# A decoder step's expert mixer: the last token block by gathered value rows in place of a dense product

## The chip, the cores and the metric

The kernel runs on one core of a Trainium2 chip. The metric is the device time of one execution in microseconds (us); the median of several runs counts. The profile's span, from the first to the last instruction, leaves out what lies around it.

## The reference, cut to what matters

One layer of a hybrid decoder: differential attention and an mLSTM mix the tokens (512 prompt tokens and 8 sample tokens), and a PEER layer follows, which is what the change touches. For each token 8 heads pick 16 of 16,384 experts each, by a product of two key halves:

```python
eidx = jnp.take_along_axis(cidx, pos, axis=-1)      # i1 * 128 + i2, 8 heads x 16
g = jax.nn.softmax(top_s, axis=-1)
ue = u[eidx]
ve = v[eidx]
act = jax.nn.gelu(jnp.einsum('nd,nhkd->nhk', xb, ue))
return jnp.einsum('nhk,nhkd->nd', g * act, ve)
```

So every token has 128 selected rows of `u` and of `v` (1024 floats each) and one weight, g * act, for each row of `v`. `v` is 16,384 x 1024 floats, 64 MB. The output is the residual plus the weighted sum of the token's 128 rows of `v`.

## The kernel before, in words

The 512 prompt tokens are two halves of 256, and each half is two blocks of 128 tokens: A0, A1, B0 and B1. For every block the kernel picks the experts (`scores`), gathers the rows of `u` one selection at a time (`gather_dot`: 128 indirect transfers from the POOL queue, each fetching one row for every token, 512 KB, with a product and sum on VectorE), and turns the dots into the weights `S` (`gelu_w`). It does not gather rows of `v`. `w_block` instead builds, for each block, the dense matrix of weights, experts x tokens, from one-hot products on VectorE, GpSimd, ScalarE and TensorE (32 groups of four tokens), into two `WT` tiles of 64 x 128 floats per partition. `v_part(j, ...)` then loads the chunk of 128 rows number j of `v` (512 KB, queue of SyncE, tag "v" with VB = 5 buffers) and multiplies the matching slice of each block's matrix with it, two matmuls of 128x512 for each block, accumulated over the 128 chunks in PSUM. With `split` False the matmuls take fp32 operands. With `split` True chunk and weights are taken apart into a rounded part and a remainder (`vh`, `vl` on ScalarE and VectorE in the buffers of `ring`; `wh`, `wl` likewise) and three products of reduced precision are summed: six matmuls for each block.

The order: chunks 0 to 127 serve A0 and A1 in fp32, and the last 28 (from JB = 100) B0 too. Beside them the `u` rows of B0 and B1 are gathered. `v_done` adds a block's PSUM sums to the residual and stores it. Then `w_block` builds B1's matrix, in the `WT` buffers that A's matrices leave, while B0 takes chunks 0 to 19 (NF = 20); chunks 20 to 99 serve B0 and B1, chunks 100 to 127 and then 0 to 19 only B1, all split. `sample_peer` is a generator whose steps (one gather or so each) are strewn among the chunks: 8 gathers of `u` rows (`urow_s`), each with a broadcast load (`xb`), then 8 gathers of `v` rows (`vrow_s`) with matmuls on 8-column weights (`py_s`); all of these tiles are in `ring`.

The engines' queues are filled by a scheduler, which simulates the program: on each engine the earliest instruction of the program that is ready in that simulation goes next. Each engine then runs its own list in order. Dependences and buffer releases become semaphore waits. `dps` holds eight PSUM banks: two for `pst_d`, two for each accumulator (`v_acc`).

Of the kernel before, what the change touches and what calls it, by code (L numbers as in the profile page):

```python
# [5 lines left out]
F32 = mybir.dt.float32  # L6
F32R = mybir.dt.float32r
BF16 = mybir.dt.bfloat16
I32 = mybir.dt.int32
U32 = mybir.dt.uint32  # L10
AF = mybir.ActivationFunctionType
ALU = mybir.AluOpType
# [3 lines left out]
P = 128  # L16
D = 1024
# [4 lines left out]
HALF = 256  # L22
# [12 lines left out]
JB = 100  # L35
# [7 lines left out]
NF = 20  # L43
# [15 lines left out]
def step_kernel(  # L59
# [7 lines left out]
    nc = tc.nc  # L67
# [8 lines left out]
    u_rows, v_rows = peer_u[0], peer_v[0]  # L76
# [24 lines left out]
    def ctile(shape, name, dt=F32, pool=None):  # L101
        return (pool or consts).tile(shape, dt, name=name)

    ident = ctile([P, P], "ident")
# [25 lines left out]
    def pst(tag):  # L130
        return ps.tile([P, 512], F32, tag=tag, name=f"ps_{tag}", bufs=PB[tag])
# [7 lines left out]
    def act(out, in_, func, scale=1.0, bias=None, accum=None):  # L139
        kw = {}  # L140
        if accum is not None:
            kw["accum_out"] = accum
        n = out.shape[0]
        b = (zero if bias is None else bias)
        nc.scalar.activation(out, in_, func, bias=b[:n, 0:1] if b.shape[0] != n else b, scale=scale, **kw)

    def copy(out, in_, scale=1.0):
        nc.scalar.activation(out, in_, AF.Copy, scale=scale)  # L148
# [6 lines left out]
    for tok, rows, sample in ((0, P, False), (P, P, False), (0, NS, True)):  # L155
        t = tp.tile([P, D], F32, tag="r4", name="xin", bufs=R4B)
# [57 lines left out]
    for i in range(2):  # L214
        scr = sp.tile([P, 64], F32, tag="w1", name="lscr", bufs=W1B)
        nc.vector.scalar_tensor_tensor(scr, lamt[:, 2 * i, :], 1.0, lamt[:, 2 * i + 1, :], op0=ALU.mult,
                                       op1=ALU.mult, accum_out=lam[:, i:i + 1])
# [7 lines left out]
    for c in range(2):  # L225
        raw = sp.tile([P, P], F32, tag="w1", name="skraw", bufs=W1B)
        nc.sync.dma_start(raw, peer_subkeys[0, c])
        p = pst("t")
# [905 lines left out]
    def w_new(*pools):  # L1134
        return [(pool.tile([P, JH, P], F32, tag="WT", name="WT", bufs=2), JH * i) for i, pool in enumerate(pools)]

    def w_prep(sel, pool, pst_):
        out = []
        for key in ("i1", "i2", "S"):
            p = pst_()  # L1140
            nc.tensor.transpose(p[:, 0:P], sel[key], ident)
            t = pool.tile([P, P], BF16 if key == "i1" else F32, tag=f"T_{key}", name=f"T_{key}", bufs=1)
            copy(t, p[:, 0:P])
            out.append(t)
            if key == "i2":
                t = pool.tile([P, P], F32, tag="T_n2", name="T_n2", bufs=1)
                copy(t, p[:, 0:P], scale=-1.0)
                out.append(t)
        return out
# [3 lines left out]
    def w_block(sel, wT, pool, pst_, no):  # L1153
        ONA, PM = ONAS[no], PMS[no]
        if not iota4:
            t = pool.tile([P, P, TG], BF16, name="iota4")
            nc.vector.tensor_copy(t, iota.unsqueeze(2).to_broadcast([P, P, TG]))
            iota4.append(t)
        i1T, i2T, ni2T, sT = w_prep(sel, pool, pst_)
        for g in range(P // TG):  # L1160
            t0 = g * TG
            tg = slice(t0, t0 + TG)
            e = pool.tile([P, P, TG], BF16, tag="ohe", name="ohe", bufs=OHE)
            nc.vector.tensor_tensor(e, iota4[0], i1T[:, tg].unsqueeze(1).to_broadcast([P, P, TG]), op=ALU.is_equal)
            a = pool.tile([P, TG, P], F32, tag="oh1", name="oh1", bufs=OH1)
            sb = sT[:, tg].unsqueeze(2).to_broadcast([P, TG, P])
            nc.gpsimd.tensor_mul(a[:, :PM], e.rearrange("p j t -> p t j")[:, :PM], sb[:, :PM])  # L1167
            if PM < TG:
                nc.vector.tensor_mul(a[:, PM:], e.rearrange("p j t -> p t j")[:, PM:], sb[:, PM:])
            b = pool.tile([P, TG, P], F32, tag="oh2", name="oh2", bufs=OHB)  # L1170
            for t in range(ONA):
                act(b[:, t, :], iota, AF.Abs, bias=ni2T[:, t0 + t:t0 + t + 1])
            if ONA:
                nc.scalar.activation(b[:, 0:ONA, :], b[:, 0:ONA, :], AF.Relu, bias=one, scale=-1.0)
            if ONA < TG:
                n = TG - ONA
                nc.vector.tensor_tensor(b[:, ONA:TG, :], iota.unsqueeze(1).to_broadcast([P, n, P]),
                                        i2T[:, t0 + ONA:t0 + TG].unsqueeze(2).to_broadcast([P, n, P]), op=ALU.is_equal)
            pw = pst_().rearrange("p (t j) -> p t j", t=TG)
            for t in range(TG):  # L1180
                nc.tensor.matmul(pw[:, t, :], b[:, t, :], a[:, t, :], start=True, stop=True)  # L1181
            for w, j0 in wT:
                copy(w[:, :, t0:t0 + TG], pw[:, :, j0:j0 + w.shape[1]].rearrange("p t j -> p j t"))
# [3 lines left out]
    for hf in range(2):  # L1187
# [24 lines left out]
        else:  # L1212
            actx.close()
            wr = ctx.enter_context(tc.tile_pool(name="wright", bufs=1, side="right"))
# [42 lines left out]
    wt = dctx.enter_context(tc.tile_pool(name="wt", bufs=1, side="right"))  # L1257
    dps = dctx.enter_context(tc.tile_pool(name="dpsum", bufs=1, space=PSUM))

    selA, selB = halves[0][0], halves[1][0]  # L1260

    def pst_d():
        return dps.tile([P, 512], F32, tag="pw", name="ps_w", bufs=2)
# [4 lines left out]
    dp = dctx.enter_context(tc.tile_pool(name="dense", bufs=2))  # L1268

    def v_acc(b):  # L1270
        return [dps.tile([P, 512], F32, tag=f"y{b}{q}", name=f"y{b}{q}") for q in range(2)]

    def v_part(j, use, split):
        vt = dp.tile([P, D], F32, tag="v", name="vtile", bufs=VB)
        nc.sync.dma_start(vt, v_rows[j * P:(j + 1) * P])
        ws = [next(w[:, j - j0, :] for w, j0 in wT if j0 <= j < j0 + w.shape[1]) for _, wT, _, _ in use]
        pairs = [((w, vt),) for w in ws]
        if split:
            vh, vl = (ring.tile([P, D], F32R, tag="g", name=n) for n in ("vh", "vl"))
            wh, wl = (dp.tile([P, 2, P], F32R, tag="wh", name=n, bufs=3) for n in ("wh", "wl"))  # L1280
            copy(vh, vt)
            nc.vector.tensor_sub(vl, vt, vh.bitcast(F32))  # L1282
            for b, w in enumerate(ws):
                copy(wh[:, b, :], w)
                nc.vector.tensor_sub(wl[:, b, :], w, wh[:, b, :].bitcast(F32))  # L1285
            pairs = [((wh[:, b, :], vh), (wh[:, b, :], vl), (wl[:, b, :], vh)) for b in range(len(ws))]
        for (py, _, j0, j1), pp in zip(use, pairs):
            for i, (lw, rv) in enumerate(pp):
                for q in range(2):
                    nc.tensor.matmul(py[q], lw, rv[:, q * 512:(q + 1) * 512],  # L1290
                                     start=(j == j0 and i == 0), stop=(j == j1 and i == len(pp) - 1))

    def v_done(tok, py):
        t = dp.tile([P, D], F32, tag="v", name="x1r", bufs=VB)
        nc.sync.dma_start(t, scr_x1[tok:tok + P])
        for q in range(2):
            nc.vector.tensor_add(t[:, q * 512:(q + 1) * 512], t[:, q * 512:(q + 1) * 512], py[q])
        nc.sync.dma_start(y_prompt[0, tok:tok + P], t)
# [59 lines left out]
    yB0 = v_acc(2)  # L1358
    useB0 = (yB0, wB0, JB % P, (JB - 1) % P)
    for j in range(JB, P):  # L1360
        v_part(j, useA + [useB0], False)
    for b in range(2):
        v_done(b * P, useA[b][0])
    wB1 = w_new(wr, wt)
    w_block(selB[1], wB1, wr, pst_d, 3)
    useB1 = (v_acc(0), wB1, NF % P, (NF - 1) % P)
    for j in range(NF):
        v_part(j, [useB0], True)
    for j in [*range(NF, P), *range(NF)]:
        v_part(j, ([useB0] if NF <= j < JB else []) + [useB1], True)  # L1370
        if j == JB - 1:
            v_done(HALF, yB0)
        if j >= SST[1] and j % SST[2] == 0:
            next(steps, None)
    for _ in steps:
        pass
    v_done(HALF + P, useB1[0])
    dctx.close()
    ctx.close()

# [30 lines left out]
```

## Time and profile before

| | us |
|---|---|
| median of 3 runs | 2348.86 |
| lowest and highest run | 2343.86 and 2352.1 |
| span of the profiled execution | 2338.3 |
| median above that span | 10.6 |
| TensorE busy in the span | 2136.7 (91%) |
| VectorE, GpSimd, ScalarE busy | 1676.6, 1247.0, 815.3 |

No device time beside its span is given for the profiled execution, so the runs stand beside it: their median is 10.6 us longer than the span. The windows view splits the span by time and tells which engine is full where. PE is TensorE's matmuls, PEld its weight loads, DVE VectorE, ACT ScalarE, POOL GpSimd, SP SyncE. An instruction's "busy" of many pipelined matmuls is the union of their spans; the distance between starts tells the pace.

### The profile page before, as it was taken

The page shows a single profiled execution, that of the slowest core. Times are in us where ns is not written, and L with a number is a line of the kernel's source. Part 1 is how long each engine was busy: PE and PEld are TensorE (multiplying, and loading weights), DVE is VectorE, ACT ScalarE, POOL GpSimd, SP SyncE. Part 2 cuts the span into 40 slices and gives each one's busy share as a digit, 9 for nine tenths or more (in the row PEclk, how much of TensorE's full clock was granted, in tenths as well). Part 3 has the DMA queues.
Part 4 walks back from the last instruction along what each step waited for, and adds up shares of the span by engine and source line. Part 5 has one row for each costly group of instructions (what it writes and reads, how often), then busy time and mean ns, then how long its engine had stood idle before and what let it go on. Part 6 is the DMA issues. An engine that isn't in the chain of part 4 may idle for free. (4 is left out here: it accounts for less than half of the span.)

```text
span 2338.3 us, 28902 instructions
## 1 busy us (share of the span) xinstructions
PE 2136.7 (91%) x8921; PEld 1528.1 (65%) x8921; DVE 1676.6 (72%) x3820; ACT 815.3 (35%) x2055; POOL 1247.0 (53%) x1118
## 2 busy tenths in 40 slices
PE   6999899889999999998979569999999997899998
PEld 4776678777878777787758454444555446777765
DVE  2355666785899878668978985664797759766667
ACT  4334233213355323333334770000122005454556
POOL 0588863551876557657785785441688636200001
PEclk9999999999989999999979669999999999999999
DMA  5687767887888989998883189997998974567678
GB/s 165 202 277 237 231 222 230 287 288 268 305 300 304 303 309 346 353 369 290 309 280 132 41 281 367 409 409 283 352 353 317 409 304 155 184 221 231 219 266 283
DMA packets 282253, 648.38 MB, mean 277 GB/s; under 512 B 29774, under 2 KB 155786, under 8 KB 282098
## 3 DMA queue, kind: packets, MB, share of 16 engines
q0 software_dynamic: 94464, 343.97, 40.9%
q1 hardware_dynamic: 187634, 302.55, 38.3%
q8 instruction: 71, 1.16, 0.2%
q14 instruction: 84, 0.69, 0.1%
HBM read 628.25 MB, written 18.18 MB: 276 GB/s over the span
## 5 line engine op out<-in xcount | busy, mean ns | idle before, releaser
L1102 POOL DMA_INDIRECT urow<-in_peer_u,k_e x512 | 621.1, 1213 | 336.8 <-DVE urow L1108 240.0
L1108 DVE SCALAR_TENSOR_TENSOR urow<-urow,xn 128x1024 f32<-128x1024 f32 x512 | 646.7, 1276 | 152.5 <-DMA urow<-in_peer_u,k_e 146.7
L1290 PE MATMUL y<-vtile,WT 128*128 128x512 f32 x1136 | 494.0, 595 | 1.7 <-ACT WT L148 0.9
L288 PE MATMUL ps_mm<-x,wch 128*128 128x264 f32 (+1 forms) x1536 | 385.3, 404 | 26.1 <-DVE sig L312 17.9
L1290 PEld LDWEIGHTS y<-vtile,WT 128*128 128x128 f32 x1136 | 215.1, 191 | 265.3 <-issue 263.5
L288 PEld LDWEIGHTS ps_mm<-x,wch 128*128 128x128 f32 x1536 | 301.0, 201 | 82.5 <-DVE sig L312 21.2
L148 ACT ACTIVATE vh<-vtile 128x1024 fp32r<-128x1024 f32 x148 | 155.6, 1057 | 228.7 <-DMA vtile<-in_peer_v 123.4
L1282 DVE TENSOR_TENSOR vl<-vtile,vh 128x1024 fp32r<-128x1024 f32 x148 | 182.7, 1240 | 39.8 <-ACT vh L148 37.8
L831 POOL TENSOR_TENSOR kpage<-kpage,qb 128x1024 f32<-128x1024 f32 x64 | 150.1, 2357 | 72.2 <-DMA qb<-scr_q 63.4
L288 PE MATMUL ps_mm<-hT,wch 128*128 128x256 f32 (+1 forms) x768 | 185.1, 392 | 1.8 <-DVE sig L312 0.9
L1167 POOL TENSOR_TENSOR oh<-ohe,T_S 128x512 f32<-128x512 bf16 (+2 forms) x128 | 148.1, 1162 | 70.9 <-ACT T_S L148 35.7
L1181 PE MATMUL ps_w<-oh,oh 128*128 128x128 f32 x768 | 122.8, 317 | 63.9 <-POOL oh L1167 29.2
L1181 PEld LDWEIGHTS ps_w<-oh,oh 128*128 128x128 f32 x768 | 113.6, 225 | 84.3 <-POOL oh L1167 63.9
L288 PEld LDWEIGHTS ps_mm<-hT,wch 128*128 128x128 f32 x768 | 144.1, 194 | 24.8 <-issue 1.3
L293 PE MATMUL ps_mm<-wch,x 128*128 128x256 f32 (+1 forms) x640 | 148.2, 382 | 0.3 <-DVE kS L690 0.3
L1290 PE MATMUL y<-vl,wh 128*128 128x512 f32 x456 | 140.2, 398 | 7.1 <-DVE vl L1282 6.1
L1290 PE MATMUL y<-vh,wh 128*128 128x512 f32 x456 | 140.1, 397 | 1.9 <-ACT vh L148 1.8
L819 POOL DMA_INDIRECT vpage<-in_cache_v,kidx x64 | 80.6, 1259 | 109.8 <-DVE vacc L897 64.2
L1290 PE MATMUL y<-vh,wl 128*128 128x512 f32 x456 | 133.3, 402 | 1.7 <-DVE wl L1285 1.7
L293 PEld LDWEIGHTS ps_mm<-wch,x 128*128 128x128 f32 (+1 forms) x640 | 106.2, 171 | 29.7 <-issue 2.4
L897 DVE SCALAR_TENSOR_TENSOR vacc<-vpage,aS,vacc 128x128 f32<-128x128 f32 x384 | 112.1, 363 | 18.7 <-DMA vpage<-in_cache_v,kidx 18.2
L148 ACT ACTIVATE WT<-ps_w 128x256 f32<-128x256 f32 x192 | 62.7, 379 | 151.6 <-PE ps_w L1181 151.6
(419 smaller groups left out, 3098.4 us busy)
## 6 DMA issues: line engine op xcount, KB each, us to landing
vtile<-in_peer_v SPq DMA_DIRECT2D x276, 512.0 KB
wch<-in_w_in SPq DMA_DIRECT2D x256, 256.0 KB
wch<-in_peer_wq SPq DMA_DIRECT2D x64, 256.0 KB
wch<-in_w_branch_a SPq DMA_DIRECT2D x32, 256.0 KB
wch<-in_w_branch_b SPq DMA_DIRECT2D x32, 256.0 KB
wch<-in_w_out SPq DMA_DIRECT2D x32, 256.0 KB
urow<-in_peer_u,k_e POOLq DMA_INDIRECT x512, 7.6
qb<-scr_q SPq DMA_DIRECT2D x8, 512.0 KB
```

Of the source, the lines that this page charges most:

```text
L148: nc.scalar.activation(out, in_, AF.Copy, scale=scale)
L288: nc.tensor.matmul(out, w[:, c0:c0 + m], xk[:, :n], start=(k == 0 and i == 0), stop=(k == KT - 1 and i == len(tt) - 1))
L293: nc.tensor.matmul(out, x[:, k, t0:t0 + m], ch[k // KP][:, k % KP, :n], start=(k == 0), stop=(k == KT - 1))
L819: nc.gpsimd.indirect_dma_start(out=t, out_offset=None, in_=rows, in_offset=bass.IndirectOffsetOnAxis(ap=kidx[:, b * 8 + pg:b * 8 + pg + 1] ...
L831: (nc.vector if KDV and pg % KDV == KDV - 1 else nc.gpsimd).tensor_mul(kt, kt, qb)
L897: nc.vector.scalar_tensor_tensor(acc[:, h, :], vt[:, h, :], wa, acc[:, h, :], op0=ALU.mult, op1=ALU.add)
L1102: nc.gpsimd.indirect_dma_start(out=gt, out_offset=None, in_=u_rows, in_offset=bass.IndirectOffsetOnAxis(ap=d["e"][:, k:k + 1], axis=0))
L1108: d["dot"] = nc.vector.scalar_tensor_tensor(gt, gt, 1.0, xn2, op0=ALU.mult, op1=ALU.mult, accum_out=d["S"][:, k:k + 1])
L1167: nc.gpsimd.tensor_mul(a[:, :PM], e.rearrange("p j t -> p t j")[:, :PM], sb[:, :PM])
L1181: nc.tensor.matmul(pw[:, t, :], b[:, t, :], a[:, t, :], start=True, stop=True)
L1282: nc.vector.tensor_sub(vl, vt, vh.bitcast(F32))
L1290: nc.tensor.matmul(py[q], lw, rv[:, q * 512:(q + 1) * 512], start=(j == j0 and i == 0), stop=(j == j1 and i == len(pp) - 1))
```

## The change

B1 gets no dense matrix. `vg_prep` clears a tile `wz` of 128 x 4096 floats, computes the expert number i1 * 128 + i2 in floats, transposes it and `S` on TensorE, and writes the transposed weights on a stride of 33 into `wz`, so that `wz` holds for each token t a 128x32 weight tile that is zero except in column t mod 32. `vg_run` makes 32 groups; a group gathers for four tokens (i, 32 + i, 64 + i, 96 + i) their 128 selected rows of `v`, one indirect transfer of 512 KB for each token, and multiplies each by the token's 128x32 weights into the 32 PSUM partitions 32j to 32j + 31, in two matmuls of 512 columns. The gathered rows go into 12 slots of 128x1024 in two slabs, which take the buffers of `WT` that A leaves, as B1's matrix did before; the first four slots' room is `wz`. B0 takes its chunks 0 to 99 alone and in fp32 (`split` False), one group after every third chunk.

```diff
+    def vg_prep(d, pool, wz):
+        nc.gpsimd.memset(wz, 0.0)
+        ef = pool.tile([P, P], F32, name="vg_ef", bufs=1)
+        nc.vector.scalar_tensor_tensor(ef, d["i1"], 128.0, d["i2"], op0=ALU.mult, op1=ALU.add)
+        p = pst_d()
+        nc.tensor.transpose(p[:, 0:P], ef, ident)
+        nc.tensor.transpose(p[:, P:2 * P], d["S"], ident)
+        eT = pool.tile([P, P], I32, name="vg_eT", bufs=1)
+        nc.vector.tensor_copy(eT, p[:, 0:P])
+        for j in range(4):
+            copy(wz[:, j * 1024:(j + 1) * 1024:33], p[:, P + 32 * j:P + 32 * j + 32])
+        return wz.rearrange("p (t c) -> p t c", c=32), eT
+
+    def vg_run(prep, py, slots):
+        wz, eT = prep
+        for i in range(32):
+            gts = []
+            for j in range(4):
+                t = 32 * j + i
+                gt = slots()
+                nc.gpsimd.indirect_dma_start(out=gt, out_offset=None, in_=v_rows,
+                                             in_offset=bass.IndirectOffsetOnAxis(ap=eT[:, t:t + 1], axis=0))
+                gts.append((j, t, gt))
+            for q in range(2):
+                for j, t, gt in gts:
+                    nc.tensor.matmul(py[q][32 * j:32 * j + 32, :], wz[:, t, :], gt[:, q * 512:(q + 1) * 512],
+                                     start=(i == 0), stop=(i == 31), skip_group_check=True)
+            yield
...
-    wB1 = w_new(wr, wt)
-    w_block(selB[1], wB1, wr, pst_d, 3)
-    useB1 = (v_acc(0), wB1, NF % P, (NF - 1) % P)
-    for j in range(NF):
-        v_part(j, [useB0], True)
-    for j in [*range(NF, P), *range(NF)]:
-        v_part(j, ([useB0] if NF <= j < JB else []) + [useB1], True)
-        if j == JB - 1:
-            v_done(HALF, yB0)
+    slab = [pool.tile([P, 8, D], F32, tag="WT", name="vslab", bufs=2) for pool in (wr, wt)]
+    slot_i = [0]
+
+    def slots():
+        i = 4 + slot_i[0] % 12
+        slot_i[0] += 1
+        return slab[i // 8][:, i % 8, :]
+
+    yB1 = v_acc(0)
+    run = vg_run(vg_prep(selB[1], dp, slab[0][:, 0:4, :].rearrange("p a c -> p (a c)")), yB1, slots)
+    for j in range(JB):
+        v_part(j, [useB0], False)
+        if j % 3 == 2:
+            next(run, None)
         if j >= SST[1] and j % SST[2] == 0:
             next(steps, None)
+    v_done(HALF, yB0)
+    for _ in run:
+        pass
     for _ in steps:
         pass
-    v_done(HALF + P, useB1[0])
+    v_done(HALF + P, yB1)
```

## Rows read from the trace of the kernel before

**Rows 1.** Windows of the last 430 us: busy us (instructions), clock, DMA share, GB/s.
```profile
1908.00:1924.00 16.00, 16.00 (x39) 7.15 (x38) 4.00 (x8) 2.73 (x4) 0.00 (x0) 1.00 0.37 125
1930.00:2010.00 80.00, 58.78 (x362) 50.28 (x363) 78.06 (x95) 43.25 (x102) 48.92 (x32) 1.00 0.42 142
2010.00:2290.00 280.00, 269.38 (x1123) 206.77 (x1122) 179.19 (x323) 147.77 (x291) 14.17 (x13) 1.00 0.71 236
2290.00:2338.30 48.30, 42.63 (x160) 27.07 (x158) 33.76 (x50) 27.82 (x45) 4.09 (x3) 0.98 0.79 279
```

**Rows 2.** Matmul groups of the whole span: records | busy us, mean ns.
```profile
L1290 PE MATMUL y<-vtile,WT 128*128 128x512 f32 x1136 | 494.0, 595 | 1.7 <-ACT WT L148 0.9 <-DMA vtile<-in_peer_v 0.8
...
L1290 PE MATMUL y<-vl,wh 128*128 128x512 f32 x456 | 140.2, 398 | 7.1 <-DVE vl L1282 6.1 <-ACT vh L148 0.9
...
L1337 PE MATMUL py_s<-vrow_s,wz 128*8 128x512 f32 x32 | 15.1, 593 | 6.1 <-DMA vrow_s<-in_peer_v,eT 6.1
```

**Rows 3.** Timeline at 2150 us, split chunks of two blocks: start, us, instruction.
```profile
2149.66 1.06 ACT L148 ACTIVATE vh<-vtile 128x1024 fp32r<-128x1024 f32 x1 [1.35 <-PE y L1290]
...
2152.46 1.06 ACT L148 ACTIVATE vh<-vtile 128x1024 fp32r<-128x1024 f32 x1 [1.34 <-PE y L1290]
```

**Rows 4.** Timeline at the end of A's chunks and the start of B1's matrix.
```profile
1913.10 0.19 PEld L1290 LDWEIGHTS y<-vtile,WT 128*128 128x128 f32 x1 [0.24 <-issue]
1913.53 0.19 PEld L1290 LDWEIGHTS y<-vtile,WT 128*128 128x128 f32 x1 [0.24 <-issue]
...
1923.83 1.02 PE L1290 MATMUL y<-vtile,WT 128*128 128x512 f32 x2
...
1926.86 0.29 DVE L1129 TENSOR_TENSOR k_S<-k_e,k_g 128x128 f32<-128x128 f32 x1
...
1929.18 0.26 ACT L148 ACTIVATE T_S<-ps_w 128x128 f32<-128x128 f32 x1
...
1930.89 1.06 ACT L148 ACTIVATE vh<-vtile 128x1024 fp32r<-128x1024 f32 x1 [1.45 <-DMA vtile<-in_peer_v]
```

**Rows 5.** Windows of two earlier stretches with gathers and chunks together.
```profile
1500.00:1600.00 100.00, 100.00 (x234) 44.27 (x233) 59.83 (x99) 0.00 (x0) 45.47 (x50) 1.00 1.03 409
1700.00:1750.00 50.00, 50.00 (x189) 28.18 (x188) 46.90 (x69) 14.51 (x48) 41.14 (x35) 1.00 0.97 352
```

**Rows 6.** DMA view of 1500 to 1600 us: queues, then issues.
```profile
q0 software_dynamic: 7012, 25.53, 63.9%
q1 hardware_dynamic: 4207, 15.32, 38.5%
...
vtile<-in_peer_v SPq DMA_DIRECT2D x29, 512.0 KB
urow<-in_peer_u,k_e POOLq DMA_INDIRECT x50, 10.7
```

**Rows 7.** Gathers of u rows and the indices they read, by line.
```profile
L1102 POOL DMA_INDIRECT urow<-in_peer_u,k_e x512: 932/976/8858, 595.1 to 1898.9; - x171
...
DMA to landing us min/median/max: 4.1/7.6/13.5
```

**Rows 8.** The line that writes the indices: first and last start.
```profile
L1018 DVE SCALAR_TENSOR_TENSOR k_e<-k_i x32: 148/167/1048, 593.8 to 1347.8; 128x16 int32<-128x16 f32 x32
```

**Rows 9.** Timeline of PE in the attention: 64-row and 128-row matmuls in turn.
```profile
158.11 0.48 PE L738 MATMUL ps_s<-kc,qn 64*128 64x128 f32 x2
158.53 0.33 PE L741 MATMUL ps_s<-bias,identr 128*128 128x128 f32 x1
158.79 0.48 PE L738 MATMUL ps_s<-kc,qn 64*128 64x128 f32 x2
...
159.37 1.41 PE L768 MATMUL ps_a<-dg,sc 128*128 128x128 f32 x8
160.62 0.68 PE L347 MATMUL ps_t<-sq,bones 128*128 128x264 f32 x2
```

**Rows 10.** Timeline of a sample matmul among the chunks.
```profile
2288.89 1.88 PE L1337 MATMUL py_s<-vrow_s,wz 128*8 128x512 f32 x4 [0.44 <-DMA vrow_s<-in_peer_v,eT]
2290.70 0.74 PE L1290 MATMUL y<-vh,wl 128*128 128x512 f32 x2
```

**Rows 11.** Timeline of the last instructions.
```profile
2329.09 1.28 DVE L1297 TENSOR_TENSOR x1r<-x1r,y 128x512 f32<-128x512 f32 x2 [3.25 <-PE y L1290]
...
2334.84 0.31 SPq L1344 DMA_DIRECT2D out_y_sample<-x1s  x1
```

**Rows 12.** GpSimd's clears at the kernel's start.
```profile
L105 POOL MEMSET ident<- 128x128 f32 x1 | 0.2, 205 | 0.3 <-POOLq L1399 0.3
...
L1399 POOL MEMSET const-float32-0.0<- 128x1 f32 x1 | 0.1, 99 | 0.3 <-issue 0.3
```

## The prediction

> **What bounds the kernel now.** I read the windows first, then the matmul groups, the timeline where A ends, and the DMA view of the gather stretch.
>
> The change works in the last 430 us, and that stretch has two parts [rows 1]. From 1930 to 2010 us VectorE is full (78 of 80 us): it builds B1's one-hot matrix while TensorE is busy for 59 us and the DMA engines for 0.42 of the time. From 2010 to 2290 us TensorE is full (269 of 280 us), and the DMA engines move 236 GB/s at a share of 0.71. So the tail is first bound by VectorE and then by TensorE; memory is not its limit.
>
> The pace of the two kinds of products is read from starts. An fp32 matmul of 512 columns leaves two records: 128 x 4 + 28 x 2 = 568 calls in the code, 1136 records [rows 2]. Their weight loads start 0.429 us apart [rows 4], so one fp32 matmul takes 0.858 us and a chunk of one block 1.716 us. A split chunk of two blocks takes 2.80 us, from one `vh` to the next [rows 3], which is 1.40 us for each block and chunk. The dense tail is 228 such (128 for B1, 100 for B0): 228 x 1.40 = 319 us. With the matrix's stretch and the sample's matmuls this fills the 414 us from the end of A (1924 us, where its last fp32 matmul ends [rows 4]) to the end.
>
> What memory can do is seen earlier: from 1500 to 1600 us, 50 gathers and 29 chunk loads run together at 409 GB/s with all 16 engines full [rows 5, 6]. 524,288 bytes by 409 GB/s are 1.282 us for one transfer of 512 KB, of either kind.
>
> **The change part by part.** Removed: `w_block` for B1 and with it some 80 us in which TensorE had B0's 20 split chunks (28 us) to do beside the matrix; B1's 128 split chunks (179 us of TensorE); 148 chunk loads' worth of `vh`/`vl` work on ScalarE and VectorE.
>
> B0's 100 chunks become fp32: 100 x 1.716 = 172 us of TensorE in place of 140, a loss of 32 us on that engine. Nothing hides it where TensorE is the bound; where transfers are, it is free. It needs no `ring` buffers, so the sample's gathers no longer queue behind them.
>
> Added on DMA: 128 gathers. After A the list is: about 96 of the 100 chunks (some four will have come by then; before, the fourth was taken up at 1930.89 [rows 4]), 128 gathers, 24 transfers of the sample (8 `urow_s`, 8 `xb`, 8 `vrow_s`), and 4 for the two `v_done` of B: 252 x 1.282 = 323 us. Before, it was 148 + 24 + 4.
>
> Their start: the gathers need the expert numbers, and these share a PSUM tile with the transpose of `S`, which is complete at 1927.15 [rows 4]. Before, the transposed `T_S` came out at 1929.2 to 1929.4 by the same steps, so the first gather goes out at about 1929.5. The clear of `wz` is 4096 floats on GpSimd; from the 128-float and the 1-float clear, (205 - 99) / 127 = 0.83 ns a float, about 3.5 us [rows 12]. It can begin when A's last tile is free and ends at about 1927, hidden behind the wait for `S`; if not, at most 3.5 us are added. The strided copies, five of 32 to 128 columns, I put at one `T_S` copy each (0.26 us), 1.3 us beside the first gathers' landing of 4.1 us at least [rows 7]. GpSimd needs 0.98 us for a gather at the median, 144 x 0.98 = 141 us: no bound. One gather lands in 7.6 us at the median and 13.5 at most [rows 7]; with 12 slots and some 9 us for a group's turn on TensorE, 128 gathers need 128 / 12 x 22.5 = 240 us by their latency, less than 323. Nor does a slot wait for its whole slab: gathers began at 595.1 us while their index tile was still being written in slices up to 1347.8 [rows 7, 8].
>
> Added on TensorE: 256 fp32 matmuls on 32 weight columns, in groups of eight. No matmul in the trace writes upper PSUM partitions beside another, so their overlap is not seen. Bounds for a group: if they do not overlap, 16 passes at the pace of the 8-column sample matmuls, (2290.70 - 2288.89) / 4 = 0.4525 us [rows 10], 7.2 us; if four run at once, a quarter of 8 x 0.858, 1.7 us. I take 9 x 0.429 = 3.9 us: passes start in order, and the second pass of one matmul must follow its first in the same columns, so only the second pass of one and the first of the next can run side by side. This is an assumption, not a row.
>
> The price of going between tile shapes can be read where 64-row matmuls alternate with 128-row ones: the 64-row pair takes 0.42 us and the next one 0.26, against 0.31 and 0.16 at the pace of eight equal 128-row records, (160.62 - 159.37) / 8 [rows 9]: 0.21 us in and out, 32 x 0.21 = 7 us. The Trainium skill, "TensorEngine Tiling (Array Packing)", Key Properties, says that changing the tiling mode drains TensorE, which speaks against strewing the groups among full-width chunks; the rows agree in sign and give the price used here. The same page's Overview has up to four times the speed at 32 columns; by that the group takes 1.7 us and the sum below would not change, as transfers bound it.
>
> TensorE's sum after 1924 us: 172 + 32 x 3.9 (124) + the sample's 32 passes x 0.4525 (14.5) + 7 + some 4 us of waiting for the first chunks = 321 us, to 2245. Transfers: 1929.5 + 323 = 2252.5. The two are 8 us apart, so transfers are the bound by a little, and TensorE's in-order list will cost some of each: I allow 5 us. At the end: one group (3.9), the residual's additions (1.3 [rows 11]), and the store, as long as from the issue of the last one to the end of the span, 2338.3 - 2334.8 = 3.5 us [rows 11]: 9 us. Span: 2252.5 + 5 + 9 = 2267, against 2338.3. The median of the runs stands 10.6 us above the span, and I carry that over: 2278 us, 71 us or 3.0% less. (A measurement of this kernel tells about 0.3%, 7 us, from no change.)
>
> DMA has a rule that speaks against this: the Trainium skill, "DMA: Bandwidth & Descriptors", Specifications, gives about 358 GB/s as the HBM limit for one core. By that 252 transfers would take 369 us and the time would be about 2324. Rows 5 and 6 disagree: 409 GB/s held for 100 us with the same mix.
>
> Stretches before 1924 us should keep their times: the change adds nothing to them, and the buffers that it takes are those that B1's matrix took.
>
> **The rivals.**
>
> *B: transfers slower, or not mixed.* Between 1700 and 1750 us the DMA engines were full (0.97) at only 352 GB/s [rows 5]: then 252 x 1.489 = 375 us, 1929.5 + 375 + 9 + 10.6 = 2324. The limit in the second rule above would come to the same. Or the planner lets B0's fp32 chunks go ahead (172 us bound by TensorE) and leaves most gathers and the sample's transfers after them (152 x 1.282 = 195 us): 1929.5 + 172 + 195 + 9 + 10.6 = 2316. For it: the queues' order is planned on a simulation. Against: the program puts a group after every third chunk, and the 12 slots let gathers run ahead.
>
> *C: the column tiles do not overlap.* Then a group is 7.2 us, TensorE's sum 172 + 232 + 14.5 + 7 + 4 = 429 us, and the end 1924 + 429 + 5 + 10.6 = 2369 us, slower by 0.9%. At the full-width pace and with no price for the shapes (6.9 us a group, 220 us) it is 2346, no change. The point from which it decides is about 7 us for a group. For it: the 8-column sample matmuls are no faster than full ones, and each group reads four different moving tiles. Against: the four matmuls write different PSUM partitions with weights in different columns.
>
> *D: the columns overlap fully.* TensorE then falls to 172 + 55 + 26 = 253 us, and the transfers bind alone: 2258 to 2272. It is within the forecast's own range.
>
> **How the numbers follow.** Forecast with D: 0.60, own range 2258 to 2300 (the upper end is a group of 5 us with both limits in each other's way). B: 0.17, 2300 to 2335. C: 0.23, of which 0.06 is within 0.3% and 0.17 slower. Faster 0.60 + 0.17 = 0.77, same 0.06, slower 0.17. The range reaches from 2256 (252 transfers at the forecast's rate with no allowance, a shorter tail) up to 2350, which takes in B and the mild end of C; about 0.05 lies below and 0.15 above.
>
> **What would show it.** Right: DMA share near 1 and about 400 GB/s from 1935 us to some 10 us before the end, TensorE at 90% or a little more; no one-hot work after 1927; `y<-vtile` pairs at 0.43 us a record; a group's eight matmuls in about 4 us. Wrong: groups of 7 us with TensorE full and DMA at 0.7 (C); DMA full at 350, or chunks first and gathers alone at the end (B); gathers that start well after 1930; any shift of the end of A from 1924 us.

## The result, and the profile after

The changed kernel takes 2289.05 us (median of 5 runs, 2279.21 to 2292.88) against 2348.86 us (5 runs): a ratio of 0.9748, 95% interval 0.972 to 0.9775, 60 us less. The forecast was 2278 with an own range of 2258 to 2300; it lies 11 us too low. The profiled execution took 2279.21 us with a span of 2277.5, so only 1.7 us lie around a span. One run in this document, of the turned kernel of experiment 6 (2327.08 us), fell in a slower state of the chip, and its median and ratio leave it out.

The same windows as in [rows 1], after the change (busy us and instructions of PE, PEld, DVE, ACT, POOL; clock; DMA share; GB/s):

```profile
1930.00:1950.00 20.00, 13.01 (x30) 3.38 (x29) 2.44 (x6) 0.00 (x0) 11.84 (x12) 0.91 1.01 396
1950.00:2050.00 100.00, 97.31 (x274) 26.36 (x275) 8.04 (x25) 1.20 (x4) 54.61 (x57) 1.00 1.03 408
2050.00:2150.00 100.00, 97.61 (x324) 27.79 (x321) 0.00 (x0) 0.00 (x0) 51.73 (x56) 1.00 1.03 409
2150.00:2200.00 50.00, 48.67 (x153) 14.74 (x151) 0.00 (x0) 0.00 (x0) 15.13 (x17) 1.00 0.94 368
2200.00:2250.00 50.00, 50.00 (x118) 22.18 (x117) 0.00 (x0) 0.00 (x0) 0.00 (x0) 1.00 0.87 304
2250.00:2277.50 27.50, 21.48 (x51) 9.18 (x49) 2.48 (x4) 0.00 (x0) 0.00 (x0) 0.93 0.72 258
```

VectorE's and ScalarE's work is gone from the tail. From 1950 to about 2180 us the DMA engines are full at 408 to 409 GB/s, as forecast. From 2200 us they are not (0.87, then 0.72), and TensorE is full: the last 80 us or so are a stretch of another kind, where the forecast had the DMA engines full to some 10 us before the end.

The matmul groups and gathers after 1930 us (records | busy us, mean ns | idle before, releasers), which stand where [rows 2] had the split products:

```profile
L1290 PE MATMUL y<-vtile,WT 128*128 128x512 f32 x397 | 185.0, 606 | 1.2 <-DMA vtile<-in_peer_v 1.2
L1318 PE MATMUL y<-vslab 128*32 128x512 f32 x512 | 138.6, 601 | 12.2 <-DMA vslab<-in_peer_v,vg_eT 12.2
L1313 POOL DMA_INDIRECT vslab<-in_peer_v,vg_eT x128 | 122.2, 955 | 106.2 <-DMA vslab<-in_peer_v,vg_eT 47.7 <-PE y L1318 22.6 <-issue 20.7
```

Of the transfers of 512 KB after 1930 us, the DMA view counts these two kinds first; with 16 of the sample's and 4 of the two `v_done` they are 245:

```profile
vtile<-in_peer_v SPq DMA_DIRECT2D x97, 512.0 KB
vslab<-in_peer_v,vg_eT POOLq DMA_INDIRECT x128, 13.3
```

138.6 us for 32 groups are 4.3 us a group, near the 3.9 of the prediction. The timeline shows that this is a coincidence (start, us, records in a row):

```profile
2055.46 1.98 PE L1290 MATMUL y<-vtile,WT 128*128 128x512 f32 x4
2057.37 1.94 PE L1318 MATMUL y<-vslab 128*32 128x512 f32 x16
2059.24 1.98 PE L1290 MATMUL y<-vtile,WT 128*128 128x512 f32 x4
2061.16 2.26 PE L1318 MATMUL y<-vslab 128*32 128x512 f32 x12
2064.08 1.90 PE L1318 MATMUL y<-vslab 128*32 128x512 f32 x4 [0.67 <-DMA vslab<-in_peer_v,vg_eT]
2065.92 1.98 PE L1290 MATMUL y<-vtile,WT 128*128 128x512 f32 x4
2067.83 1.90 PE L1318 MATMUL y<-vslab 128*32 128x512 f32 x4
2069.67 1.98 PE L1290 MATMUL y<-vtile,WT 128*128 128x512 f32 x4
2071.58 1.92 PE L1318 MATMUL y<-vslab 128*32 128x512 f32 x8
2073.43 1.98 PE L1290 MATMUL y<-vtile,WT 128*128 128x512 f32 x4
```

A token is four records. Where none waits for a gather, four tokens together (x16) take 1.87 us to the next start, two (x8) 1.85, one (x4) 1.84: the column tiles overlap in full, and a token alone costs as much as four. The scheduler strews single tokens between the chunks, and the tokens of a longer run come apart when their gathers land one after another (12 records from 2061.16 to 2064.08 us); both raise the average to 4.3. A chunk beside a token takes 1.91 us in place of 1.716. And twelve tokens go by while five chunks do; the program has nine chunks to twelve tokens. So the gathers are done early, as the end of the timeline and of the chain of waits show:

```profile
2189.69 1.98 PE L1290 MATMUL y<-vtile,WT 128*128 128x512 f32 x4
2191.61 2.43 PE L1318 MATMUL y<-vslab 128*32 128x512 f32 x12
2193.97 77.52 PE L1290 MATMUL y<-vtile,WT 128*128 128x512 f32 x180
```

```profile
2136.43 14.60 DMA vslab<-in_peer_v,vg_eT
2158.17 14.60 DMA vslab<-in_peer_v,vg_eT
2194.04 72.31 PE y L1290 x168
2266.37 4.50 DMA x1r<-scr_x
```

In the chain a gather's landing stands every 21.7 us: 12 gathers and 5 chunks, 17 x 1.282 = 21.8 us, so this part is bound by transfers. After 2194 us TensorE has 45 chunks left (180 records in 77.52 us, 1.72 us a chunk), and the DMA engines wait for it.

### The profile page after: what moved, and what is told of

Read it like the earlier page. It is cut to its first block, busy times and chain, and to the rows that moved or that the text cites. A ratio compares the mean times of both kernels' runs of the same rounds, so it can differ in the third digit from the quotient of the medians.

```text
span 2277.5 us, 26092 instructions
## 1 busy us (share of the span) xinstructions
PE 2098.4 (92%) x8208; PEld 1349.4 (59%) x8208; DVE 1403.7 (62%) x3382; ACT 593.5 (26%) x1615; POOL 1327.5 (58%) x1215
## 4 chain that ended last, share of the span: by engine, by line
PE 44%; DVE 11%; DMA 10%; issue 7%; POOL 5%; ACT 1%; DVEq 0%; POOLq 0%; ACTq 0%
PE y L1290 20%; PE ps_mm L288 9%; DMA vslab<-in_peer_v,vg_eT 6%; DVE urow L1108 3%; POOL urow L1102 3%; PE ps_mm L293 3%; PE y L1318 3%; PE ps_s L738 2%; DMA urow<-in_peer_u,k_e 1%; PE ps_w L1181 1%; POOL oh L1167 1%; PE ps_s L741 1%; DVE tk_w L975 1%; DVE ohe L1164 1%; DMA vpage<-in_cache_v,kidx 1%
## 5 line engine op out<-in xcount | busy, mean ns | idle before, releaser
L1102 POOL DMA_INDIRECT urow<-in_peer_u,k_e x512 | 632.2, 1235 | 326.9 <-DVE urow L1108 223.3
L1290 PE MATMUL y<-vtile,WT 128*128 128x512 f32 x1536 | 680.6, 598 | 3.0 <-DMA vtile<-in_peer_v 2.1
L1290 PEld LDWEIGHTS y<-vtile,WT 128*128 128x128 f32 x1536 | 286.6, 191 | 382.5 <-issue 377.8
L1313 POOL DMA_INDIRECT vslab<-in_peer_v,vg_eT x128 | 122.2, 955 | 106.2 <-DMA vslab<-in_peer_v,vg_eT 47.7
L1318 PE MATMUL y<-vslab 128*32 128x512 f32 x512 | 138.6, 601 | 12.2 <-DMA vslab<-in_peer_v,vg_eT 12.2
L1181 PE MATMUL ps_w<-oh,oh 128*128 128x128 f32 x512 | 88.3, 336 | 46.0 <-POOL oh L1167 29.2
L1181 PEld LDWEIGHTS ps_w<-oh,oh 128*128 128x128 f32 x512 | 81.4, 242 | 62.3 <-POOL oh L1167 45.5
L1167 POOL TENSOR_TENSOR oh<-ohe,T_S 128x384 f32<-128x384 bf16 (+2 forms) x96 | 96.4, 1011 | 12.7 <-ACT T_S L148 5.6
L1318 PEld LDWEIGHTS y<-vslab 128*32 128x32 f32 x512 | 30.7, 109 | 112.0 <-issue 88.5
L832 DVE TENSOR_REDUCE sK<-kpage 128x16 f32<-128x1024 f32 x64 | 77.1, 1210 | 26.3 <-POOL kpage L831 26.2
```

The source lines that it names most:

```text
L1102: nc.gpsimd.indirect_dma_start(out=gt, out_offset=None, in_=u_rows, in_offset=bass.IndirectOffsetOnAxis(ap=d["e"][:, k:k + 1], axis=0))
L1290: nc.tensor.matmul(py[q], lw, rv[:, q * 512:(q + 1) * 512], start=(j == j0 and i == 0), stop=(j == j1 and i == len(pp) - 1))
L1313: nc.gpsimd.indirect_dma_start(out=gt, out_offset=None, in_=v_rows, in_offset=bass.IndirectOffsetOnAxis(ap=eT[:, t:t + 1], axis=0))
L1318: nc.tensor.matmul(py[q][32 * j:32 * j + 32, :], wz[:, t, :], gt[:, q * 512:(q + 1) * 512], start=(i == 0), stop=(i == 31), skip_group_che ...
```

## The experiments

Kernels that were measured together share the runs of the kernel before on the same chip; kernels of different chips are compared by these ratios.

**1. Do the column tiles overlap?** All four tokens of a group go to one column tile, so that none can overlap.

```diff
-                    nc.tensor.matmul(py[q][32 * j:32 * j + 32, :], wz[:, t, :], gt[:, q * 512:(q + 1) * 512],
-                                     start=(i == 0), stop=(i == 31), skip_group_check=True)
+                    nc.tensor.matmul(py[q][0:32, :], wz[:, t, :], gt[:, q * 512:(q + 1) * 512],
+                                     start=(i == 0 and j == 0), stop=(i == 31 and j == 3), skip_group_check=True)
```

> The changed kernel, but all four tokens of a group add into PSUM partitions 0 to 31 (B1's sums thus fall into 32 rows and its other rows are left out), so that no two of a group's matmuls lie in different columns of the array. If running side by side is what makes the gathered product cheap, a group takes 16 passes of 0.43 to 0.45 us, 6.9 to 7.2 us, in place of about 1.9 when all four rows are there; TensorE is then the bound from 1928 us: 100 x 1.716 + 32 x 7.1 + 14 = 413 us, and the span is 2345 to 2360. If transfers are the bound whatever TensorE does, the span stays below 2290.

Measured: 2376.62 us, ratio 1.0094 (1.0057 to 1.0131); the profiled span, 2365.8, is 6 us above the expected top. Its windows and timeline:

```profile
2050.00:2150.00 100.00, 100.00 (x221) 29.86 (x220) 0.00 (x0) 0.00 (x0) 26.22 (x28) 1.00 0.82 281
2150.00:2250.00 100.00, 100.00 (x227) 32.01 (x226) 0.00 (x0) 0.00 (x0) 26.22 (x28) 1.00 0.84 295
```

```profile
2100.45 4.48 PE L1318 MATMUL y<-vslab 128*32 128x512 f32 x10
2104.86 1.98 PE L1290 MATMUL y<-vtile,WT 128*128 128x512 f32 x4
2106.77 2.76 PE L1318 MATMUL y<-vslab 128*32 128x512 f32 x6
```

Ten records take 4.41 us, 0.44 each, so 16 take 7.1. TensorE is full and the DMA engines at 0.82. This is rival C of the prediction, near its price (2369): without the overlap the change loses its whole gain, some 88 us.

**2. What does the matrix alone cost?** The kernel before, without the building of B1's matrix; B1 is multiplied with B0's.

```diff
-    wB1 = w_new(wr, wt)
-    w_block(selB[1], wB1, wr, pst_d, 3)
-    useB1 = (v_acc(0), wB1, NF % P, (NF - 1) % P)
+    useB1 = (v_acc(0), wB0, NF % P, (NF - 1) % P)
```

> The kernel before without building B1's matrix: B1's chunks are multiplied with B0's matrix instead (so B1's output is not its own). If what the change saves is the stretch in which the matrix is built, the dense tail alone takes 228 x 1.40 = 319 us and some 20 us of sample and ends from 1924 us: a span of 2265 to 2280, as short as with gathers. If the saving came from the cheaper product by gathered rows, the span stays near 2320.

Measured: 2304.92 us, ratio 0.9783 (0.973 to 0.9836). The ratio makes it 51 us less (39 to 63); the two medians, 2304.92 and 2348.03, are 43 us apart. The profiled span, 2300.3, lies between the two expectations. Taken off first, the matrix is thus most of what the change saves (60 us). But what is left takes longer than by the prediction's terms (319 us for the split products, 14.5 for the sample's matmuls, 9 for the end, 343 together): it runs from 1930 to 2300 us. Where chunks serve one block alone, no engine is quite full (PE 101, DVE 78, ACT 65 of 110 us):

```profile
2190.00:2300.00 110.00, 101.09 (x381) 65.65 (x379) 77.79 (x115) 65.45 (x107) 10.18 (x7) 0.98 0.80 278
```

**3. What do B1's gathers cost?** The changed kernel without B1's gathers and matmuls; B1 gets B0's sums.

```diff
-        if j % 3 == 2:
-            next(run, None)
...
-    v_done(HALF + P, yB1)
+    v_done(HALF + P, yB0)
```

> The changed kernel without B1's gathers and matmuls (B1's output gets B0's sums; B1's own part is left out). B0's chunks are then bound by TensorE: from 1928 us 100 x 1.716 = 172, 14 for the sample's matmuls and some 8 to the end: a span of about 2120, so that B1's gathers cost 155 to 165 us, near 128 x 1.282 = 164. If gathers were mostly hidden behind B0's chunks, the span would stay above 2180.

Measured: 2145.58 us (two runs), so B1's gathers cost 2289.13 - 2145.58 = 143.5 us, less than the 155 to 165 expected. The span, 2143.0, is 23 us above the expected 2120: until 1965 us TensorE waits for chunk loads, 13.7 us in seven waits, of which the first and the longest are shown. 128 gathers at 1.282 us would be 164. The difference is room that the chunks leave: from 1997 us on they are bound by TensorE, as the timeline of this kernel ends,

```profile
1937.09 1.98 PE L1290 MATMUL y<-vtile,WT 128*128 128x512 f32 x4 [2.75 <-DMA vtile<-in_peer_v]
...
1947.33 6.49 PE L1290 MATMUL y<-vtile,WT 128*128 128x512 f32 x8 [4.75 <-DMA vtile<-in_peer_v]
...
1997.39 139.32 PE L1290 MATMUL y<-vtile,WT 128*128 128x512 f32 x324
```

81 chunks at 1.72 us, with 1.28 for the transfer of one. Over all 100 chunks 0.44 us each are, as an estimate, 44 us of free transfer time, of which the changed kernel uses 164 - 143.5 = 20.

**4. fp32 or split for B0?** B0's 100 chunks stay split (`wh`, `wl` narrowed to one block).

```diff
-            wh, wl = (dp.tile([P, 2, P], F32R, tag="wh", name=n, bufs=3) for n in ("wh", "wl"))
+            wh, wl = (dp.tile([P, len(ws), P], F32R, tag="wh", name=n, bufs=3) for n in ("wh", "wl"))
...
-        v_part(j, [useB0], False)
+        v_part(j, [useB0], True)
```

> The changed kernel, but B0's 100 chunks stay in the split form (six matmuls of 0.233 us, with the rounding on ScalarE and VectorE) as before. If TensorE alone sets the pace of the tail, its 45 chunks run at 1.40 us in place of 1.72 and the span is 12 to 15 us shorter, 2263 to 2266. If the plain form costs nothing, the span is the same; if the rounding and its buffers bring back the waits for ring buffers, it is longer, 2285 or more.

Measured: 2315.68 us, ratio 0.9827 (0.9786 to 0.9867), 27 us more than the changed kernel, measured on another chip. This is the third case of the expectation. The faster products bring nothing: `vh` and `vl` take the `ring` buffers, the sample's last gathers wait 4 to 27 us each for work on the chunks (two are shown), and all of the sample's `v` rows come after 2211 us, where no engine is full:

```profile
2219.05 1.02 POOL L1348 DMA_INDIRECT urow_s<-in_peer_u,eT  x1 [27.42 <-PE y L1290]
...
2263.51 0.97 POOL L1363 DMA_INDIRECT vrow_s<-in_peer_v,eT  x1 [13.82 <-DVE vl L1282]
```

```profile
2211.00:2302.00 91.00, 77.47 (x273) 46.29 (x271) 63.17 (x105) 49.86 (x81) 10.56 (x10) 0.98 0.82 295
```

So fp32 for B0, 32 us dearer on TensorE by the prediction's sum, is right here.

**5. Where are the 11 us beyond the forecast?** The scheduler's order is undone: each group is tied on TensorE behind its third chunk, and its tokens are taken last gathered first.

```diff
+    last_v = [None]
...
-                    nc.tensor.matmul(py[q], lw, rv[:, q * 512:(q + 1) * 512],
+                    last_v[0] = nc.tensor.matmul(py[q], lw, rv[:, q * 512:(q + 1) * 512],
...
-                for j, t, gt in gts:
+                for j, t, gt in reversed(gts):
+                  with tc.issue_after(last_v[0].ins):
```

> The changed kernel with one more rule for the planner: a group's matmuls come on TensorE behind the third chunk that stands before it in the program, and its four tokens are taken last gather first, so that all eight matmuls stand together. If the 20 us over the sum of transfers are the tail of 45 chunks that TensorE does alone (1.72 us each against 1.28 for a transfer), chunks and gathers now end together: 245 transfers x 1.282 = 314 us from 1930, the span 2255 to 2265 and DMA full to its end. If the order is indifferent because the sum of TensorE's work or the transfers' latency set the end, it stays at 2275 to 2290.

Measured: 2271.69 us, ratio 0.9632 (0.9586 to 0.9677). With 1.7 us taken off, that is a span of 2270.0, above the expected 2255 to 2265; the profiled span is 2283.9. The order was run again beside the unaltered changed kernel:

> The changed kernel as it is, beside the next runs on one chip. The ratio should come out at 0.975 again, and its TensorE should again show chunks and single tokens in turn and a tail of some 45 chunks alone.

> The same ordered kernel, now beside the changed kernel on one chip. If the order is worth what the profile of its first run showed (332 us in place of 348 from the first gather to the end), its median is 12 to 18 us under the changed kernel's. If the first run was only a faster chip, the two medians agree within 5 us.

Measured: 2289.13 us, ratio 0.9711 (0.9665 to 0.9757), and 2264.85 us, ratio 0.9619 (0.9573 to 0.9665): 24 us less on the same chip, more than the expected 12 to 18 (experiment 6 finds 15.6 of it in the tail). The ordered kernel beats both kernels. The windows of its second profile:

```profile
2050.00:2150.00 100.00, 93.55 (x324) 31.74 (x322) 0.00 (x0) 0.00 (x0) 43.21 (x46) 1.00 1.03 409
2150.00:2200.00 50.00, 46.71 (x158) 15.89 (x159) 0.00 (x0) 0.00 (x0) 20.66 (x22) 1.00 1.03 409
2200.00:2250.00 50.00, 45.89 (x160) 15.12 (x159) 0.00 (x0) 0.00 (x0) 17.85 (x19) 1.00 1.03 409
```

The DMA engines stay full up to 2250 us, and TensorE is busy for 92 to 94% of the time: nothing is left over for the end. By the reckoning of experiment 3, B1's gathers cost 2264.85 - 2145.58 = 119 us here, 45 less than 164, and the estimated 44 us of free transfer time are used up.

**6. Place or turn?** Two kernels with half of that edit each: the turned order of tokens alone, and the place behind the third chunk alone.

> Only the order of a group's four tokens is turned round; the groups keep their place in the program and the planner is free to put them anywhere. Theory (the loss against ordered lies in where the planner puts the groups: gathers first, 45 chunks alone at the end, TensorE-bound at 1.72 us): nothing changes in that, so 2280 to 2295 us, as the changed kernel, with a last stretch of 40 or more chunks alone. Rival (the strewn tokens themselves, one or two at 1.84 us where four would take 1.87, are the loss, and taking the last gathered token first lets the group run as one): groups of 16 records, TensorE work of the gathers down from 138 to about 60 us, and 2260 to 2272 us.

> Only the place of the groups is fixed (each behind its third chunk on TensorE); the four tokens are multiplied in the order in which they were gathered. Theory (place alone makes the gain): 2262 to 2275 us, DMA engines at 1.0 and about 409 GB/s until some 15 us before the end, no stretch of chunks alone. Rival (tokens must also be taken last first, so that TensorE waits once for a group and not for each of its tokens): TensorE waits several times in a group, each for the next gather's landing, and the time is 2275 to 2290 us.

Measured: the turn alone 2285.18 us, ratio 0.9725 (0.9689 to 0.9761), its timeline ending on 44 chunks alone; the place alone 2273.28 us, ratio 0.9676 (0.9645 to 0.9707). The end of the turned kernel's timeline, then a group of the placed kernel:

```profile
2210.34 75.80 PE L1290 MATMUL y<-vtile,WT 128*128 128x512 f32 x176
```

```profile
2109.29 1.07 PE L1321 MATMUL y<-vslab 128*32 128x512 f32 x6
2111.23 1.90 PE L1321 MATMUL y<-vslab 128*32 128x512 f32 x10 [0.87 <-DMA vslab<-in_peer_v,vg_eT]
```

The profiled executions reach the tail at different times, so the tail itself is compared: from the start of the first gather to the end of the span.

| kernel | first gather | end of span | between |
|---|---|---|---|
| changed | 1929.9 | 2277.5 | 347.6 |
| changed, again | 1943.7 | 2292.0 | 348.3 |
| turned alone | 1944.2 | 2292.1 | 347.9 |
| placed alone | 1954.9 | 2286.9 | 332.0 |
| ordered | 1951.5 | 2283.9 | 332.4 |
| ordered, again | 1939.5 | 2272.1 | 332.6 |

Three and three agree within 0.7 us: the place is worth 15.6 us, the turn nothing. In the placed kernel a group runs 6 records, waits once for a gather, and then goes on at once with the other 10; what TensorE waits for there is hidden behind the transfers. The rival of the second expectation falls. The ordered kernel's groups mostly show the same 6 and 10 records, so the turn did not let all eight matmuls stand together, as its expectation had meant.

**7. Is the tail then bound by transfers, and would a shorter list help?** The ordered kernel with `JB`, the chunk from which B0 joins A's blocks, at 112 (12 chunks more for B0 alone) and at 88 (12 fewer).

```diff
-JB = 100
+JB = 112
```

> The ordered kernel with JB at 112: B0 takes part in 16 of A's chunks in place of 28, which takes 12 x 1.716 = 21 us from TensorE before A ends and adds 12 chunk loads, 15 us of transfers, behind it. If the stretch before A's end is bound by TensorE and the one behind it by transfers, the sum is 5 us less. If transfers are what binds both stretches, it is up to 15 us more. (An estimate from the chunk's 1.716 us and the transfer's 1.282.)

```diff
-JB = 100
+JB = 88
```

> As ordered, but B0 takes 12 more chunks (88 to 99) beside A's blocks, so that 12 chunks fewer are loaded after A. Theory (transfers bind the stretch after A, at 1.28 us for one): 12 x 1.28 = 15 us less there. Before it TensorE gets 12 x 1.72 = 21 us more; in the windows of before from 1500 to 1900 us TensorE shows busy all the time but waits for transfers in part of it (DMA share 1.03 at 1500 to 1600 and 1.02 at 1800 to 1900, 0.82 at 1600 to 1700). If transfers bind that stretch too, the 21 us are hidden in part: 2250 to 2266 us in all. Rival (TensorE is the bound of the stretch with A): the 21 us show there in full and the time is 2266 to 2280 us.

Measured: 2286.32 us, ratio 0.9705 (0.9654 to 0.9755), for 112, DMA share 1.03 up to 2250 us: 21 us above the ordered kernel measured with it, where 12 x 1.28 = 15 were put as the most. Its timeline ends on 16 chunks alone, in place of the ordered kernel's four:

```profile
2253.67 27.73 PE L1292 MATMUL y<-vtile,WT 128*128 128x512 f32 x64
```

The 32 groups are used up after 96 chunks. So 12 chunks more stand behind the last group, at 0.44 us over a transfer each: by this estimate 5 us that the expectation left out. Nor are the 12 transfers in the tail. From the first gather on, 97 chunk loads and 245 transfers are left, as with 100, and the tail takes 2287.5 - 1950.4 = 337.1 us, 5 more than in the table. A's end comes earlier, but the first gather waits for B1's weights: the clear of `wz` starts at 1912.5 us, the weights are complete at 1947.9, and the gather starts at 1950.4. Part of the 21 us is a difference between executions. From the first chunk load of `v` (1356.4 us) to the end this profile takes 931.1 us, the two ordered ones 921.7 and 920.5: 10 us more.

With 88 it is 2288.82 us, ratio 0.9739 (0.9702 to 0.9776): slower than both expectations. Its tail is the shorter for 26 transfers fewer, 2272.2 - 1979.5 = 292.7 us. But its first gather comes 638 us after the first chunk load (1341.5 us), in place of 586 to 589 in the ordered and placed kernels, and from that load to the end it takes 930.7 us. The profile shows a third cause (waits of 1700 to 1800 us: engine, line, waited for, us, times, longest; then the timeline):

```profile
PEld ps_w L1181 <- POOL oh L1167: 24.0, 14, 3.7
...
PE ps_w L1181 <- POOL oh L1167: 19.8, 14, 3.5
```

```profile
1736.17 3.60 PE L1292 MATMUL y<-vtile,WT 128*128 128x512 f32 x8
1740.88 1.16 PE L1181 MATMUL ps_w<-oh,oh 128*128 128x128 f32 x8 [1.11 <-POOL oh L1167]
...
1786.73 13.56 PE L1292 MATMUL y<-vtile,WT 128*128 128x512 f32 x24 [0.64 <-ACT WT L148]
```

From 1740 to 1786 us TensorE has no chunk to multiply: the chunks from 88 on need B0's matrix, which is still being built (VectorE busy for 44 and GpSimd for 42 of these 46 us). With `JB` at 100 A's chunks fill that time (TensorE busy all of 1700 to 1800 us, against 79 here). The same window with 88, then in the second ordered profile:

```profile
1740.00:1786.00 46.00, 25.68 (x113) 21.73 (x113) 44.22 (x57) 15.93 (x48) 41.65 (x33) 0.63 0.72 216
```

```profile
1740.00:1786.00 46.00, 46.00 (x167) 25.28 (x167) 38.72 (x64) 12.09 (x40) 39.55 (x32) 1.00 0.96 357
```

So transfers bind the tail, but a shorter list behind A does not help: what leaves it costs as much or more ahead of it.

## Why the prediction was right

**The bound of the tail, before.** VectorE first, then TensorE: held. The split between them was not: the matrix alone gives 43 to 51 us (experiment 2), less than the 80 us of its stretch, since what is left without it takes some 370 us in place of the 343 of the prediction's terms. Those count TensorE alone. TensorE stands idle for 16 of the 370 us, 9 of them where split chunks serve one block; where the rest of the 27 us goes is not shown.

**The start.** The weights were complete at 1928.2 us (1927.15 before), the clear took 3.51 us (3.5 forecast) from 1924.22, and the first gather went out at 1929.87 (1929.5 forecast). That a slot need not wait for its whole slab held. The row quoted for it was misread in part: its 32 writes serve four blocks, and 1347.8 is the last one of the second half, not of the tile that the gathers of 595.1 us read.

**The transfers.** 245 after 1930 us, not 252 (16 of the sample's in place of 24, 97 chunks in place of 96), at 408 to 409 GB/s: 1.282 us each, as [rows 5] had it, for 200 us on end. The Trainium skill's limit of about 358 GB/s for a core ("DMA: Bandwidth & Descriptors", Specifications) is not seen here, nor rival B's slow rate. The Trainium skill, "Perfetto Trace Analysis", Roofline, calls the 358 GB/s a core's share when both cores of a pair draw, and puts the practical ceiling of a core that is active alone at about 120% of it; the run lies under that (409 / 358 = 114%).

**The group on TensorE.** The assumption that "passes start in order" and so only one pass hides was wrong: four tokens take 1.87 us, near the lower bound of 1.7 us. The Trainium skill, "TensorEngine Tiling (Array Packing)", Overview, gives up to four times the speed where the small dimension is at most 32; the runs agree, as 7.1 us without the overlap against 1.87 is 3.8 times. A group takes 0.15 us and the chunk beside it 0.19 more than four passes of 0.429, so 0.35 in and out where the prediction had 0.21. The same page of the Trainium skill, Key Properties, says that a change of tiling mode drains TensorE; that fits, but no run here shows that the drain is what the 0.35 us are. Both errors were hidden where transfers bind. Rival C's milder sum, 2346, leaves out the 5 us of the end that the sum before it has; with them it is 2351.

**Each in the other's way: the term that was too small.** "I allow 5 us" for what TensorE's in-order list costs. By transfers alone, 245 x 1.282 = 314 us from the first gather, the list would have been done at 2244; the last addition began at 2270.98, 27 us later. The scheduler let the gathers run ahead of B0's chunks, 12 to 5 in place of 12 to 9, and left 45 chunks to TensorE alone at 1.72 us. Rival B had looked at the opposite order, chunks first; this way round had not been priced. Putting the groups back in the program's places removes 15.6 us of it (experiment 6). By the prediction's own terms 245 transfers give 314 + 5 + 9 = 328 us from the first gather to the end; the changed kernel takes 347.6 and the ordered one 332.4. So the allowance of 5 us was nearly right for groups in the program's places, and 20 us short in total for the order that the scheduler made; the last 4 us no run here takes apart.

**From span to time, and luck.** The 10.6 us that the forecast carried over from before are no fixed part of a run: around a span lie 1.7 us, and the rest is a difference between executions. The profiled span of before makes 2340.0 us with 1.7 added, less than all five of its runs, and the profiled execution of after is the lowest of its five; that the median again stood 11.5 us above the span was luck (in the second profile of the changed kernel it stood 2.9 us below). The sum of 2267 us for the span stands against 2277.5 measured, 10 us too low, and that is the 11 us between forecast and median. It would have been 20 had the transfers been counted right: the 7 too many made good 9 us of the allowance that was too small. From the first chunk load of `v` (1342.9 us before, 1344.9 and 1359.1 after) to the end, the profile before takes 995.4 us and the two of the changed kernel 932.6 and 932.9: 63 us less, where the forecast's spans differ by 71.

The executions differ upstream of the change: first gathers from 1929.9 to 1944.2 us in three profiles of kernels that are alike up to there (changed, changed again, turned). At the first gather of `u` rows they already stand apart, at 597.5, 607.2 and 604.0 us, and the granted clock of 200 to 300 us is 0.95, 0.85 and 0.86. The first two, in that order:

```profile
200.00:300.00 100.00, 87.98 (x389) 63.61 (x388) 70.56 (x79) 32.31 (x81) 77.30 (x48) 0.95 0.69 228
```

```profile
200.00:300.00 100.00, 94.69 (x384) 66.31 (x384) 55.60 (x73) 32.48 (x84) 75.76 (x47) 0.85 0.64 212
```

Open: whether that clock is the cause of the whole difference and what lowers it, and how much of the 21 us with `JB` at 112 is such a difference (experiment 7).

## What to carry to other kernels

Where transfers bind a stretch, look at what the queues' order leaves for its end: work that is slower on its engine than in its transfer must be spread evenly, or it stands alone at the end; a share of DMA that falls from 1.03 to 0.87 while TensorE goes to full shows it at once. Column-tiled matmuls pay by the group, not by the token: one 32-column matmul costs what four cost (1.84 us against 1.87 here), so where TensorE is the bound the four must come together; where transfers bind, as here, only their place among the chunks mattered. Compare executions from an event of the stretch itself (here the first gather) when something upstream wanders by more than the effect.

## What the runs showed that was not expected

- Four column tiles in fp32 overlap in full: 16 records in 1.87 us against 1.84 for 4. In what order the halves of the tokens stand in TensorE's list within such a run no view shows. The sample's 8-column matmuls ran beside them as well: from 2022.86 to 2024.60 us, 8 records of `y<-vslab` and 4 of `py_s` alternate in 1.74 us.
- GpSimd waited before gathers for earlier gathers to land (47.7 us in 32 waits), with 9.7 to 18.3 us from issue to landing, which the prediction had not counted among a gather's waits. With 12 slots it bound nothing while gathers ran: from 1950 to 2150 us the DMA engines stayed full.
- With `JB` at 88 the granted clock is 1.00 from 1700 to 1740 us and 0.63 from 1740 to 1786, where TensorE was busy for 25.7 of 46 us with waits of up to 3.5 us between; with 100 it is 1.00 through that time. Eight matmuls of 128 columns took 1.16 us at the start of the stretch and mostly 2.06 to 2.08 us later in it, 1.8 times as long, which is toward the ratio of the levels of 2.4 and 1.2 GHz.
